# Scaling attention probabilities with one table of factors, and reading compression tokens at a stride

## The chip, the cores and the metric

The kernel runs on one core of one Trainium2 chip. The metric is device time of one execution, in microseconds (us); the text compares medians of several runs. The kernel is one program of about 16,000 instructions on five engines: TensorE (PE, with its weight loads listed apart as PEld), VectorE (DVE), ScalarE (ACT), GpSimd (POOL) and SyncE (SP), which issues most of the transfers.

## What is computed

Two layers of a transformer on 256 tokens of width 1024, in float32. The first layer mixes with a gated recurrence (HGRN2), the second with a sparse attention (NSA) whose keys and values come from a shared projection; each is followed by a gated feed-forward network. The change touches the second layer only, in two places:

```python
# compression of keys and values: blocks of 32 tokens, a new one every 16
r = t.reshape(B, S // CMP_STRIDE, CMP_STRIDE, NSA_KV_HEADS, NSA_HEAD_DIM)
blocks = jnp.concatenate([r[:, j:j + n_cmp] for j in range(n_sub)], axis=2)
blocks = blocks + pos[None, None, :, None, :]
flat = blocks.transpose(0, 1, 3, 2, 4).reshape(B, n_cmp, NSA_KV_HEADS, CMP_BLOCK * NSA_HEAD_DIM)
return jax.nn.silu(flat @ w1) @ w2
...
# attention: three branches, each a softmax, weighted by gates
g = g.reshape(B, Q_BLOCK, N_BRANCH, NSA_KV_HEADS, NSA_GROUP)[..., None]
o = g[:, :, 0] * o_c + g[:, :, 1] * o_s + g[:, :, 2] * o_w
```

With 256 tokens there are 15 compressed blocks for each of four key heads, and the selected and the windowed branch see all tokens up to the query's.

## The kernel before

Activations are held transposed, 128 features by 256 tokens. A float32 product is made of three TensorE products: every weight tile and every activation is split into a rounded part (`wh`, `hh`, written by ScalarE) and a remainder (`wl`, `hl`, written by VectorE at L308 and L480), and L484, L485 and L486 add `hh*wh`, `hl*wh` and `hh*wl`. So TensorE can start a weight tile only when ScalarE has copied it and VectorE has subtracted, 1024 columns at a time.

Weights stream through four buffers of 1 MB (`raw`), issued by SyncE in a fixed list; a buffer is loaded again when its last reader is done. The order of everything else comes from a scheduling framework, which places instructions on each engine by priorities and its own estimates; on the chip each engine then runs its list strictly in that order.

The second layer (`nsa`) goes as follows. Two projections make the tokens that are compressed (kind 0 keys, kind 1 values) and two more the selected and windowed keys `KR`. Then the list `ORDER["nsa"]` runs: `c` is compression, `q` a query projection (`nq`, four of them, into `QR`), `G` the gates, `n` the norm of two query projections (sums `hs`, a root made by ACT and DVE in turns into `hry` and `hrt`, then the products `hb`), `w` values, `x` the compressed branch's softmax (`css`, its transpose `pct`), `s` the scores of one pair of heads, `v` that pair's values, `a` parts of a modulation product.

The lines that the change touches are these. `cmp_blocks` (L1072 on) turns a projection into `Z`, 128 partitions by four heads by 128, then adds position vectors and stores blocks in `D`, one contiguous column group of 64 (four heads by 16 blocks) for each of 16 token offsets; column 15 of each head is cleared. `compress` (L1094 on) multiplies each such group as weights with 256 columns of `raw` (L1103), in two halves, kinds 0 and 1 on two halves of the array; each half frees its two `raw` buffers. `attend_scores` makes for each of eight pairs `j` two tiles `Pt` (one for each head of the pair): L1213 adds the mask and takes the maximum, ACT takes the exponential in eight instructions (L429), L1225 and L1227 make the factors `cf`, L1231 scales. `attend_values` transposes `Pt` on TensorE (`ptt`, L1246), copies it (L1249, L1251) and multiplies with the values (`po`, L1263).

Of the kernel before, what the change touches and what calls it, by code (L numbers as in the profile page):

```python
# [10 lines left out]
F32 = mybir.dt.float32  # L11
# [5 lines left out]
ALU = mybir.AluOpType  # L17
# [3 lines left out]
P = 128  # L21
S = 256
D = 1024
# [8 lines left out]
PTS = 3  # L32
# [164 lines left out]
class K:  # L197
# [767 lines left out]
    def nsa(self):  # L965
        nc = self.nc
        with self.tc.tile_pool(name="ns", bufs=1) as sp, self.tc.tile_pool(name="ns2", bufs=2) as s2, \
# [17 lines left out]
            KR = sp.tile([P, 2, 2, S], F32, name="KR")  # L985
            V = sp.tile([P, 2, 2, 256], F32, name="V")
            self.KR, self.V = KR, V
            Dt = [sp.tile([P, 16, 64], F32, tag=f"D{i}", name=f"D{i}") for i in range(2)]
            with self.tc.tile_pool(name="nsk", bufs=1) as sk:
                dk = []  # L990
                for kind in range(2):
# [18 lines left out]
                for kind in range(2):  # L1010
                    self.cmp_blocks(*dk[kind], kind, Dt[kind], sk)
                hk = self.full_pair(0, "kv", xr, s2, KACT)
            self.s3 = self.late.enter_context(self.tc.tile_pool(name="nsp", bufs=2 * PTS))
            self.QR = sp.tile([P, 8, S], F32, name="QR")

            self.QN, self.O = {}, None
# [18 lines left out]
            for t in ORDER["nsa"]:  # L1035
                n = int(t[1:] or 0)
# [22 lines left out]
            for i in range(4):  # L1059
                ws = self.fetch("nsa_out", i)  # L1060
                ps = self.acc_tile(f"nso{i}")
# [9 lines left out]
    def cmp_blocks(self, sw, u, kind, Dt, pool):  # L1071

        nc = self.nc
        Z = pool.tile([P, 4, P], F32, tag="Z", bufs=1, name=f"Z{kind}")
        for m in range(2):
            for hh in range(2):
                for par in range(2):
                    src = u[hh * 64:hh * 64 + 64, m].rearrange("p (t two) -> p two t", two=2)[:, par]
                    dst = Z[par * 64:par * 64 + 64, 2 * m + hh]
                    b = sw[hh * 64:hh * 64 + 64, m:m + 1]  # L1080
                    if par == 0:
                        nc.scalar.activation(dst, src, AF.Identity, bias=b)
                    else:
                        nc.vector.tensor_scalar_add(dst, src, b)
        nc.gpsimd.memset(Dt.rearrange("p i (h c) -> p i h c", h=4)[:, :, :, 15:16], 0.0)
        zv = Z.rearrange("p h (a r) -> p r h a", r=8)
        for half in range(2):
            d = Dt[:, 8 * half:8 * half + 8].rearrange("p i (h c) -> p i h c", h=4)[:, :, :, 0:15]
            pos = self.col(f"pos{kind}")[:, 8 * half:8 * half + 8][:, :, None].to_broadcast([P, 8, 15])
            for h in range(4):  # L1090
                nc.vector.tensor_tensor(d[:, :, h], zv[:, :, h, half:half + 15], pos, op=ALU.add)

    def compress(self, Dt):
        nc, tp = self.nc, self.tp  # L1094
        ps = self.m_tile([P, 256], "cmp1")
        for half in range(2):
            if half:
                yield
            raw = [self.fetch_raw("w1", 2 * half + kind) for kind in range(2)]
            w = [t.rearrange("p (i c) -> p i c", i=8) for _, t in raw]  # L1100
            for i in range(8):
                for kind in range(2):
                    nc.tensor.matmul(ps[64 * kind:64 * kind + 64], lhsT=Dt[kind][:, 8 * half + i], rhs=w[kind][:, i],  # L1103
                                     start=half == 0 and i == 0, stop=half == 1 and i == 7,
                                     tile_position=(0, 64 * kind))
            for n, _ in raw:
                self.release_raw(n)
        hid = self.pt_tile("hid")[:, :256]
        self.sigmoid(hid, ps, [P, 256])
        nc.vector.tensor_tensor(hid, ps, hid, op=ALU.mult)  # L1110
        self.cmp_tail(hid)
        yield
# [82 lines left out]
    def attend_scores(self, j):  # L1195
        nc, s2 = self.nc, self.s2
        g = j // 4
        mx = s2.tile([P, 8], F32, tag="mx", name="mx")
        sm = s2.tile([P, 8], F32, tag="sm", name="sm")
        Pt = [self.s3.tile([P, 2, 384], F32, tag="Pt", name=f"Pt{j}_{h}") for h in range(2)]  # L1200
        self.Pt[j] = Pt
        cs = self.c("caus")
        for tt, (o, n) in enumerate(((0, P), (P, S))):

            ps = [self.m_tile([P, 2, n], f"s{tt}") for _ in range(2)]
            for half in range(2):
                hs = slice(64 * half, 64 * half + 64)
                nc.tensor.matmul(ps[half], lhsT=self.QR[hs, j, tt * P:tt * P + P], rhs=self.KR[hs, g, :, 0:n],  # L1208
                                 start=True, stop=True)
            for br in range(2):  # L1210
                for half in range(2):
                    i = half * 4 + br * 2 + tt
                    nc.vector.tensor_tensor_reduce(out=Pt[half][:, br, o:o + n], in0=ps[half][:, br], in1=cs[:, S - n:],  # L1213
                                                   scale=1.0, scalar=-3e38, op0=ALU.add, op1=ALU.max,
                                                   accum_out=mx[:, i:i + 1])
        nm = s2.tile([P, 8], F32, tag="nm", name="nm")
        nc.vector.tensor_scalar_mul(nm, mx, -0.125)  # L1217
        for br in range(2):
            for half in range(2):
                for tt, (o, n) in enumerate(((0, P), (P, S))):  # L1220
                    i = half * 4 + br * 2 + tt
                    self.act(Pt[half][:, br, o:o + n], Pt[half][:, br, o:o + n], AF.Exp, scale=0.125,
                                         bias=nm[:, i:i + 1], accum_out=sm[:, i:i + 1])
        cf = s2.tile([P, 2, 2, 2], F32, tag="cf", name="cf")
        nc.vector.reciprocal(cf.rearrange("p a b c -> p (a b c)"), sm)  # L1225
        for tt in range(2):
            nc.vector.tensor_tensor(cf[:, :, :, tt], cf[:, :, :, tt], self.G[:, tt, j, :, 1:3], op=ALU.mult)  # L1227
        for br in range(2):
            for half in range(2):
                for tt, (o, n) in enumerate(((0, P), (P, S))):  # L1230
                    nc.vector.tensor_scalar_mul(Pt[half][:, br, o:o + n], Pt[half][:, br, o:o + n],  # L1231
                                                cf[:, half, br, tt:tt + 1])

    @first("av")
    def attend_values(self, j):
# [149 lines left out]
```

## Time and profile before

| what | value |
|---|---|
| median of three runs | 758.28 us (756.89 to 758.37) |
| profiled execution, its own time | 757.06 us |
| span of its profile | 755.3 us |
| TensorE busy | 727.8 us, 96% of the span |
| VectorE busy | 572.4 us, 76% |
| ScalarE busy | 394.9 us, 52% |
| mean TensorE clock granted | 0.993 of full |

Times below are us from the start of the span. A row of the timeline gives start, length, engine, line, operation, output and inputs with the number of instructions merged; in brackets stands how long the engine sat idle before, and what released it. Successive instructions of one engine overlap a little, so that one row's length is more than the step to the next row's start; the step is what an instruction costs in a busy queue.

### The profile page before, as it was taken

How to read it: one execution, taken by the hardware profiler on the slowest of the kernel's cores; microseconds unless marked ns; L12 is line 12 of the kernel's file. 1: busy time of each engine (PE TensorE's matmuls, PEld its weight loads, DVE VectorE, ACT ScalarE, POOL GpSimd, SP SyncE). 2: the span in 40 equal slices, each digit the busy share in tenths (PEclk: the TensorE clock that was granted, in tenths of full speed). 3: DMA queues.
4: the chain of work that ended last, by engine and by line, in shares of the span. 5: the costliest groups of instructions: out<-in, count | busy, mean ns of one | idle time of the engine just before them, and what ended most of it. 6: DMA issues, size and time to landing. Idle time of an engine off the chain costs nothing.

```text
span 755.3 us, 15991 instructions
## 1 busy us (share of the span) xinstructions
PE 727.8 (96%) x6580; PEld 663.9 (88%) x6580; DVE 572.4 (76%) x1231; ACT 394.9 (52%) x746; POOL 0.6 (0%) x7
## 2 busy tenths in 40 slices
PE   4999999899999999999999899999999999999997
PEld 2999986689999999999997787554799999999997
DVE  6996988459899898887679888679589657565641
ACT  4339856357645544544465654568566544544330
POOL 0000000000000000000000000000000000000000
PEclk9999999799999999999999999999999999999999
DMA  8999735375489797886744843453764646765700
GB/s 342 336 344 357 275 128 212 126 285 209 164 288 377 284 357 266 338 328 260 292 139 133 315 161 111 168 201 141 279 228 158 223 167 229 273 209 194 272 31 22
DMA packets 26571, 174.13 MB, mean 231 GB/s; under 512 B 3201, under 2 KB 4609, under 8 KB 6018
## 3 DMA queue, kind: packets, MB, share of 16 engines
q1 hardware_dynamic: 24912, 170.80, 61.6%
q10 hardware_dynamic: 1586, 2.32, 1.1%
q8 instruction: 51, 0.84, 0.4%
q14 instruction: 22, 0.18, 0.1%
HBM read 170.48 MB, written 1.05 MB: 227 GB/s over the span
## 4 chain that ended last, share of the span: by engine, by line
PE 88%; DVE 5%; ACT 3%; DMA 2%; issue 1%; ACTq 0%; DVEq 0%
PE ff L486 11%; PE ff L485 11%; PE ff L484 11%; PE ffo L484 6%; PE ffo L485 5%; PE ffo L486 5%; PE po L1263 3%; PE adapsss L385 2%; PE ptt L1246 2%; DVE wl L308 2%; PE s L1208 1%; PE adapsg L385 1%; PE q L485 1%; PE nso L484 1%; PE hg_i L748 1%
## 5 line engine op out<-in xcount | busy, mean ns | idle before, releaser
L308 DVE TENSOR_TENSOR wl<-raw,wh 128x1024 fp32r<-128x1024 f32 x201 | 243.7, 1220 | 71.9 <-ACT wh L307 71.6
L307 ACT CAST wh<-raw 128x1024 fp32r<-128x1024 f32 x201 | 208.4, 1048 | 155.4 <-PE ff L485 56.9
L486 PE MATMUL ff<-hh,wl 128*128 128x256 f32 (+1 forms) x704 | 198.3, 282 | 0.0
L485 PE MATMUL ff<-hl,wh 128*128 128x256 f32 (+1 forms) x704 | 198.1, 282 | 0.0
L484 PE MATMUL ff<-hh,wh 128*128 128x256 f32 (+1 forms) x704 | 198.1, 282 | 0.0
L486 PEld LDWEIGHTS ff<-hh,wl 128*128 128x128 f32 x704 | 133.1, 189 | 0.0
L485 PEld LDWEIGHTS ff<-hl,wh 128*128 128x128 f32 x704 | 132.7, 189 | 0.3
L484 PEld LDWEIGHTS ff<-hh,wh 128*128 128x128 f32 x704 | 132.6, 189 | 0.1
L484 PE MATMUL ffo<-gh,wh 128*128 128x256 f32 x352 | 99.4, 283 | 0.7 <-DVE x L638 0.7
L486 PE MATMUL ffo<-gh,wl 128*128 128x256 f32 x352 | 98.7, 281 | 0.8 <-DVE wl L308 0.8
L485 PE MATMUL ffo<-gl,wh 128*128 128x256 f32 x352 | 98.6, 280 | 0.0
L359 DVE CUSTOM_DVE_ANT_0 junk<-raw,crep 128x1024 f32<-128x1024 f32 x64 | 78.0, 1219 | 5.2 <-DMA raw<-in_w 4.6
L484 PEld LDWEIGHTS ffo<-gh,wh 128*128 128x128 f32 x352 | 66.1, 188 | 1.8 <-DVE x L638 1.5
L486 PEld LDWEIGHTS ffo<-gh,wl 128*128 128x128 f32 x352 | 66.1, 188 | 1.0 <-DVE wl L308 1.0
L485 PEld LDWEIGHTS ffo<-gl,wh 128*128 128x128 f32 x352 | 66.1, 188 | 0.0
L479 ACT CAST gh<-fg 128x256 fp32r<-128x256 f32 x44 | 17.8, 405 | 41.8 <-DVE fg L894 41.2
L429 ACT ACTIVATE Pt<-Pt,nm 128x128 f32<-128x128 f32 x64 | 28.2, 442 | 9.8 <-DVE nm L1217 9.8
L480 DVE TENSOR_TENSOR gl<-fg,gh 128x256 fp32r<-128x256 f32 x44 | 18.5, 421 | 8.2 <-ACT gh L479 8.2
L587 ACT ACTIVATE hh<-t,mod 128x256 fp32r<-128x256 f32 x24 | 11.3, 505 | 21.3 <-DVE t L586 21.3
L385 PE MATMUL adapsss<-raw,c 128*32 128x512 f32 x128 | 21.0, 629 | 1.0 <-issue 1.0
L429 ACT ACTIVATE fs<-ff 128x256 f32<-128x256 f32 x38 | 14.4, 379 | 14.1 <-PE ff L486 14.1
L638 DVE SCALAR_TENSOR_TENSOR x<-ffo,mod,x 128x256 f32<-128x256 f32 x16 | 7.7, 480 | 18.4 <-PE ffo L486 18.4
(322 smaller groups left out, 1463.8 us busy)
## 6 DMA issues: line engine op xcount, KB each, us to landing
raw<-in_w SPq DMA_DIRECT2D x160, 1024.0 KB, 6.2
x<-in_x SPq DMA_DIRECT2D x2, 512.0 KB, 4.9
usq<-huq ACTq DMA_DIRECT2D x16, 64.0 KB, 2.4
out<-x SPq DMA_DIRECT2D x8, 128.0 KB, 1.9
cst<-in_cst ACTq DMA_DIRECT2D x1, 558.0 KB, 6.6
usk<-huk ACTq DMA_DIRECT2D x8, 64.0 KB, 4.1
raw<-in_w SPq DMA_DIRECT2D x1, 512.0 KB, 4.3
rselr<-in_rsel SPq DMA_DIRECT2D x1, 256.0 KB, 2.8
```

The source lines that it names most:

```text
L307: nc.scalar.copy(wh, u)
L308: nc.vector.tensor_tensor(wl, u, wh.bitcast(F32), op=ALU.subtract)
L359: nc.vector.tensor_tensor_reduce(out=junk, in0=t[:, h * D:(h + 1) * D], in1=self.crep, scale=1.0, scalar=0.0, op0=ALU.mult, op1=ALU.add, a ...
L385: nc.tensor.matmul(self.aps[32 * j:32 * j + 32, :q], lhsT=self.c32[:, k], rhs=t[:, n * D + j * q:n * D + (j + 1) * q], start=k == 0, stop= ...
L429: r = nc.scalar.activation(out, in_, func, **kw)
L479: self.nc.scalar.copy(hi, v)
L480: self.nc.vector.tensor_tensor(lo, v, hi.bitcast(F32), op=ALU.subtract)
L484: mm(ps, lhsT=wh, rhs=hh, start=first, stop=False)
L485: mm(ps, lhsT=wh, rhs=hl, start=False, stop=False)
L486: mm(ps, lhsT=wl, rhs=hh, start=False, stop=last)
L1246: nc.tensor.transpose(pt[:, e], Pt[half][:, br, e * P:(e + 1) * P], self.c("ident"))
L1263: nc.tensor.matmul(po[64 * half:64 * half + 64, t], lhsT=w[:, half], rhs=rhs, start=n == 0, stop=n == len(steps) - 1, tile_position=(0, 64 ...
```

## The change

Three edits. Positions are added to whole rows of tokens: `Z` plus a position vector repeated over 64 groups of eight tokens, 128x512 at a time, once for each half, so that `D` holds all tokens in their order and nothing is cleared any more. The weights of the compression products are then taken from `D` by an access pattern, 64 columns that lie eight floats apart, the second half starting eight floats on. And the two `Pt` tiles of a pair become one, of which VectorE multiplies each branch in a single `tensor_tensor` with a small table of factors (two heads by three column blocks, repeated over 128 columns); the pool holds three of these tiles instead of six of half the size.

```diff
-            Dt = [sp.tile([P, 16, 64], F32, tag=f"D{i}", name=f"D{i}") for i in range(2)]
+            Dt = [sp.tile([P, 2, 512], F32, tag=f"D{i}", name=f"D{i}") for i in range(2)]
...
-            self.s3 = self.late.enter_context(self.tc.tile_pool(name="nsp", bufs=2 * PTS))
+            self.s3 = self.late.enter_context(self.tc.tile_pool(name="nsp", bufs=PTS))
...
-        nc.gpsimd.memset(Dt.rearrange("p i (h c) -> p i h c", h=4)[:, :, :, 15:16], 0.0)
-        zv = Z.rearrange("p h (a r) -> p r h a", r=8)
         for half in range(2):
-            d = Dt[:, 8 * half:8 * half + 8].rearrange("p i (h c) -> p i h c", h=4)[:, :, :, 0:15]
-            pos = self.col(f"pos{kind}")[:, 8 * half:8 * half + 8][:, :, None].to_broadcast([P, 8, 15])
-            for h in range(4):
-                nc.vector.tensor_tensor(d[:, :, h], zv[:, :, h, half:half + 15], pos, op=ALU.add)
+            pos = self.col(f"pos{kind}")[:, 8 * half:8 * half + 8][:, None, :].to_broadcast([P, 64, 8])
+            nc.vector.tensor_tensor(Dt[:, 1 - half].rearrange("p (a r) -> p a r", r=8),
+                                    Z.rearrange("p h (a r) -> p (h a) r", r=8), pos, op=ALU.add)
+
+    def block_cols(self, Dt, half, i):
+
+        return bass.AP(tensor=Dt.tensor, offset=Dt.offset + (8 if half else 512) + i,
+                       ap=[list(Dt.ap[0]), [P, 4], [8, 16]])
...
-                    nc.tensor.matmul(ps[64 * kind:64 * kind + 64], lhsT=Dt[kind][:, 8 * half + i], rhs=w[kind][:, i],
+                    nc.tensor.matmul(ps[64 * kind:64 * kind + 64], lhsT=self.block_cols(Dt[kind], half, i), rhs=w[kind][:, i],
...
-        Pt = [self.s3.tile([P, 2, 384], F32, tag="Pt", name=f"Pt{j}_{h}") for h in range(2)]
-        self.Pt[j] = Pt
+        PT = self.s3.tile([P, 2, 2, 384], F32, tag="Pt", name=f"Pt{j}")
+        Pt = self.Pt[j] = [PT[:, h] for h in range(2)]
...
-        cf = s2.tile([P, 2, 2, 2], F32, tag="cf", name="cf")
-        nc.vector.reciprocal(cf.rearrange("p a b c -> p (a b c)"), sm)
-        for tt in range(2):
-            nc.vector.tensor_tensor(cf[:, :, :, tt], cf[:, :, :, tt], self.G[:, tt, j, :, 1:3], op=ALU.mult)
+
+        rs = s2.tile([P, 2, 2, 2], F32, tag="rs", name="rs")
+        nc.vector.reciprocal(rs.rearrange("p a b c -> p (a b c)"), sm)
+        cf = s2.tile([P, 2, 2, 3], F32, tag="cf", name="cf")
+        for tt, e in ((0, 1), (1, 2)):
+            sh = [P, 2, 2, e]
+            nc.vector.tensor_tensor(cf[:, :, :, tt:tt + e], rs[:, :, :, tt:tt + 1].to_broadcast(sh),
+                                    self.G[:, tt, j, :, 1:3, None].to_broadcast(sh), op=ALU.mult)
         for br in range(2):
-            for half in range(2):
-                for tt, (o, n) in enumerate(((0, P), (P, S))):
-                    nc.vector.tensor_scalar_mul(Pt[half][:, br, o:o + n], Pt[half][:, br, o:o + n],
-                                                cf[:, half, br, tt:tt + 1])
+            v = PT[:, :, br].rearrange("p h (e t) -> p h e t", e=3)
+            nc.vector.tensor_tensor(v, v, cf[:, :, br, :, None].to_broadcast([P, 2, 3, P]), op=ALU.mult)
```

The scheduling framework places the instructions of the second layer anew. On VectorE, ahead of the first query's remainders (`wl_0_5340` before, `wl_0_5326` now), nothing is taken out but the eight position additions of kind 0, for which two now stand; behind them, both remainders stand ahead of the last `u` (L630), of which one stood ahead and one behind. Three other places matter below.

On VectorE behind the compression products: `sg` and `hid` are the sigmoid of the compression's hidden layer, `wl_0` of `raw_5337` (now `raw_5323`) belongs to the gates, that of `raw_5347` (now `raw_5333`) to the second query. Before:

```order
L470 TENSOR_SCALAR sg<-cmp_5318 128x256
L940 TENSOR_TENSOR QR<-QR,usq_5402 128x512
L308 TENSOR_TENSOR wl_0_5485<-raw_5337,wh_0_5484 128x1024
L480 TENSOR_TENSOR hl_5280<-t_5305,hh_5279 128x256
L480 TENSOR_TENSOR hl_5280<-t_5309,hh_5279 128x256
L308 TENSOR_TENSOR wl_0_5529<-raw_5347,wh_0_5528 128x1024
L474 TENSOR_SCALAR hid<-hid 128x256
L308 TENSOR_TENSOR wl_1_5533<-raw_5347,wh_1_5532 128x1024
L475 RECIPROCAL hid<-hid 128x256
```

And now:

```order
L470 TENSOR_SCALAR sg<-cmp_5304 128x256
L308 TENSOR_TENSOR wl_0_5471<-raw_5323,wh_0_5470 128x1024
L939 SCALAR_TENSOR_TENSOR usq_5388<-usq_5388,cols,cst 128x512
L474 TENSOR_SCALAR hid<-hid 128x256
L940 TENSOR_TENSOR QR<-QR,usq_5388 128x512
L475 RECIPROCAL hid<-hid 128x256
L308 TENSOR_TENSOR wl_0_5515<-raw_5333,wh_0_5514 128x1024
L476 TENSOR_TENSOR hid<-hid,sg 128x256
```

The reciprocal has moved ahead of the second query's remainder.

On TensorE among the products of the first values `v` (weights 0 and 1 alternate, twelve products each): `gt` is the transposed gate table, `hs` the sums of the first and second query. Before:

```order
L748 MATMUL v_5699<-wh_1_5704,hh_5279 128x256
L749 MATMUL v_5699<-wl_1_5705,hh_5279 128x256
L750 MATMUL v_5699<-wh_1_5704,hl_5280 128x256
L748 MATMUL v_5699<-wh_1_5704,hh_5279 128x256
L1162 MATMUL gt<-cst,gu 128x128 x2
L950 MATMUL hs<-hsqq_5400,cst 32x256 x2
L950 MATMUL hs<-hsqq_5589,cst 32x256 x2
L749 MATMUL v_5699<-wl_1_5705,hh_5279 128x256
```

And now:

```order
L748 MATMUL v_5679<-wh_0_5680,hh_5265 128x256
L950 MATMUL hs<-hsqq_5386,cst 32x256 x2
L749 MATMUL v_5679<-wl_0_5681,hh_5265 128x256
L750 MATMUL v_5679<-wh_0_5680,hl_5266 128x256
L748 MATMUL v_5679<-wh_0_5680,hh_5265 128x256
L749 MATMUL v_5679<-wl_0_5681,hh_5265 128x256
L950 MATMUL hs<-hsqq_5575,cst 32x256 x2
L750 MATMUL v_5679<-wh_0_5680,hl_5266 128x256
```

The sums have moved from the fourth group of twelve (behind 40 products) into the first (the last of them behind 11).

On TensorE where the scores begin: `pct` is the transpose of the compressed branch's probabilities, `s` the first scores. Before:

```order
L748 MATMUL v_5943<-wh_1_5948,hh_5279 128x256
L749 MATMUL v_5943<-wl_1_5949,hh_5279 128x256
L750 MATMUL v_5943<-wh_1_5948,hl_5280 128x256
L748 MATMUL v_5943<-wh_1_5948,hh_5279 128x256
L1191 MATMUL pct<-cst,css 128x128 x2
```

And now:

```order
L748 MATMUL v_5917<-wh_0_5918,hh_5265 128x256
L749 MATMUL v_5917<-wl_0_5919,hh_5265 128x256
L1193 MATMUL pct<-cst,css 128x128 x2
L1210 MATMUL s_5646<-KR,QR 128x256
L1210 MATMUL s_5647<-KR,QR 128x256
```

Before, 16 products of the second values stood ahead of `pct`; now eight do.

## Rows read from the trace of the kernel before

**Rows 1.** The page: busy time by engine, and the chain that ended last, by engine.

```profile
PE 727.8 (96%) x6580; PEld 663.9 (88%) x6580; DVE 572.4 (76%) x1231; ACT 394.9 (52%) x746; POOL 0.6 (0%) x7
...
PE 88%; DVE 5%; ACT 3%; DMA 2%; issue 1%; ACTq 0%; DVEq 0%
```

**Rows 2.** Busy time of each engine in stretches of the second layer: length, then PE, PEld, DVE, ACT, POOL busy (instructions), granted clock, DMA share, GB/s.

```profile
400.00:410.00 10.00, 8.13 (x59) 6.44 (x58) 9.87 (x24) 5.17 (x15) 0.00 (x0) 1.00 0.18 36
...
420.00:430.00 10.00, 7.64 (x60) 6.10 (x57) 7.34 (x13) 8.20 (x15) 0.00 (x0) 1.00 0.99 394
...
440.00:450.00 10.00, 8.20 (x71) 7.41 (x70) 7.07 (x19) 5.40 (x11) 0.00 (x0) 1.00 0.26 106
...
480.00:535.00 55.00, 54.96 (x388) 29.04 (x377) 40.27 (x184) 33.97 (x117) 0.00 (x0) 1.00 0.59 219
```

**Rows 3.** TensorE's timeline at the places where it waits, from several answers.

```profile
407.30 0.39 PE L486 MATMUL nq<-hh,wl 128*128 128x256 f32 x1 [1.87 <-DVE wl L308]
...
413.62 0.40 PE L959 MATMUL hb<-hry,rsel 128*128 128x256 f32 x2
...
415.43 7.12 PE L1103 MATMUL cmp<-raw,D 128*64 128x256 f32 x62
...
424.10 0.39 PE L484 MATMUL gates<-hh,wh 128*128 128x256 f32 x1 [1.56 <-ACT wh L307]
...
425.36 0.38 PE L486 MATMUL gates<-hh,wl 128*128 128x256 f32 x1 [0.75 <-DVE wl L308]
...
447.96 0.50 PE L959 MATMUL hb<-hry,rsel 128*128 128x256 f32 x2 [1.80 <-ACT hry L479]
...
472.99 0.55 PE L1246 MATMUL ptt<-cst,Pt 128*128 128x128 f32 x3 [0.45 <-ACT V L1032]
```

**Rows 4.** Groups of instructions of the stretch 400 to 560, by line and shape: out and in, count, busy us, mean ns of one, idle before.

```profile
L1091 DVE TENSOR_TENSOR D<-Z,cols 128x120 f32<-128x120 f32 x13 | 4.3, 373 | 0.0
...
L961 DVE TENSOR_TENSOR QR<-QR,hb 128x512 f32<-128x512 f32 x4 | 2.7, 681 | 0.0
...
L1181 DVE TENSOR_TENSOR css<-css,cmx 128x256 f32<-128x256 f32 x2 | 0.8, 419 | 0.0
...
L1231 DVE TENSOR_SCALAR Pt<-Pt,cf 128x256 f32<-128x256 f32 x32 | 11.1, 347 | 0.0
...
L1231 DVE TENSOR_SCALAR Pt<-Pt,cf 128x128 f32<-128x128 f32 x32 | 9.0, 281 | 0.0
...
L1103 PEld LDWEIGHTS cmp<-raw,D 128*64 128x64 f32 x64 | 4.7, 137 | 2.4
...
L484 PEld LDWEIGHTS nq<-hh,wh 128*128 128x128 f32 x64 | 12.1, 189 | 1.1 <-issue 0.8 <-ACT wh L307 0.3
```

**Rows 5.** VectorE's timeline around the first query's remainders.

```profile
402.12 0.37 DVE L1091 TENSOR_TENSOR D<-Z,cols 128x120 f32<-128x120 f32 x1
402.41 0.74 DVE L938 SCALAR_TENSOR_TENSOR KR<-huk,cols,cst 128x512 f32<-128x512 f32 x1
...
406.03 1.22 DVE L308 TENSOR_TENSOR wl<-raw,wh 128x1024 fp32r<-128x1024 f32 x1
407.16 0.42 DVE L630 TENSOR_TENSOR u<-k,rstd 128x256 f32<-128x256 f32 x1
...
411.72 0.41 DVE L460 SCALAR_TENSOR_TENSOR hrt<-hs,hrt 128x256 f32<-128x256 f32 x1
```

**Rows 6.** SyncE's queue where the gates' and the second query's weights are issued, and ScalarE's copy that waits for the first of them.

```profile
418.71 0.87 SPq L287 DMA_DIRECT2D raw<-in_w  x2
...
423.00 1.05 ACT L307 CAST wh<-raw 128x1024 fp32r<-128x1024 f32 x1 [1.65 <-DMA raw<-in_w]
```

**Rows 7.** VectorE's timeline at the second query's first remainder and the reciprocal behind it.

```profile
427.20 1.22 DVE L308 TENSOR_TENSOR wl<-raw,wh 128x1024 fp32r<-128x1024 f32 x1 [1.07 <-ACT wh L307]
...
429.68 1.75 DVE L475 RECIPROCAL hid<-hid 128x256 f32<-128x256 f32 x1
```

**Rows 8.** The root of the first two queries: sums on TensorE, ScalarE's first and last step, and a step of VectorE that stands in its queue between.

```profile
441.14 0.64 PE L950 MATMUL hs<-hsqq,cst 128*32 128x256 f32 x8
...
441.85 0.47 ACT L429 ACTIVATE hry<-hs,eps 128x256 f32<-128x256 f32 x1 [0.24 <-PE hs L950]
...
444.06 0.75 DVE L939 SCALAR_TENSOR_TENSOR usq<-usq,cols,cst 128x512 f32<-128x512 f32 x1 [1.87 <-DMA usq<-huq]
...
447.50 0.41 ACT L479 CAST hry<-hrr 128x256 fp32r<-128x256 f32 x1 [2.66 <-DVE hrr L463]
```

**Rows 9.** The start of the scores: TensorE's second values, `pct` and the second pair's scores, ScalarE's first exponential and the copy of `V` behind the sixteenth; and, in the fifth pair or so, VectorE's scaling and the transposes that follow it.

```profile
458.99 0.28 PE L748 MATMUL v<-wh,hh 128*128 128x256 f32 x1
...
460.94 0.44 PE L1191 MATMUL pct<-cst,css 128*128 128x128 f32 x2
...
464.46 1.78 PE L1208 MATMUL s<-KR,QR 64*128 64x512 f32 x4 [0.68 <-DVE mx L1213]
...
465.34 0.40 ACT L429 ACTIVATE Pt<-Pt,nm 128x128 f32<-128x128 f32 x1 [5.06 <-DVE nm L1217]
...
472.37 0.56 ACT L1032 COPY V<-v 128x512 f32<-128x512 f32 x1
...
516.76 1.92 DVE L1231 TENSOR_SCALAR Pt<-Pt,cf 128x128 f32<-128x128 f32 x8
...
517.46 1.27 PE L1246 MATMUL ptt<-cst,Pt 128*128 128x128 f32 x9
```

## The prediction

> **What bounds the kernel now.** The page comes first: TensorE is busy for 96% of the span and the chain that ended last lies on it for 88% [rows 1]. So an edit counts only where TensorE waits, or if it makes a TensorE instruction longer. The table by stretches shows where it has something to gain: some 2 us of every ten are idle around 400, 420 and 440, all at a granted clock of 1.00, while from 480 to 535 it is busy for 54.96 of 55 us [rows 2]. TensorE's timeline then names each wait of that part [rows 3]: 1.87 us for the first query's remainder `wl`; at the gates 1.56 for ScalarE's `wh` and 0.75 for `wl`; 1.80 at 447.96 for the root `hry`; and 0.45 at 472.99 for ScalarE's copy of `V`. Last come the timelines of the engines waited for [rows 5 to 9].
>
> I follow the shift of TensorE against its own place before (minus is earlier) through these waits. What an instruction costs in a full queue is its length less about 0.08: 373 ns at 402.12 makes a step of 0.29 [rows 5].
>
> **First query.** Eight additions ahead of its remainder go out (8 × 0.29 = 2.34 us) and two come in. The trace has no addition of this form on `Z`; a tensor-tensor of 128x512 takes 681 ns, a step of 0.60 [rows 4], so 1.20 comes in. The old ones at 373 ns read every eighth float; a dense 120 elements would take about 280 ns, by the line through 256 elements in 419 and 512 in 681 (1.02 ns an element and 0.157) [rows 4]. The new ones read densely, and 0.60 is a fair value (bounds: 0.55, and 0.95 at the strided 1.8 ns an element). VectorE is busy for 9.87 of ten us there [rows 2], so `wl` moves from 406.03 to about 404.9 and TensorE goes on 1.15 earlier, still after a wait of 0.7.
>
> More than half of that is given back. Behind `wl` now stand the other remainder, `u`, two additions, `KR`, `usk`, `KR` and two instructions of 128x256: 1.13 + 0.34 + 1.20 + 0.66 + 0.66 + 0.60 + 0.67 = 5.3 us to the root's step `hrt`, where 4.56 lay between (407.16 to 411.72) [rows 5]. That step comes at 411.3, only 0.45 earlier, and the products `hb` at 413.62 [rows 3], which need what follows it, can't move by more than about 0.5. **Shift −0.5.**
>
> **Compression.** The 64 weight columns now lie 32 bytes apart. No weight load of the trace is like that. Before, 62 passes take 7.12 us, 0.115 each, behind loads of 137 ns [rows 3, 4], so the loads are hidden. Below: nothing changes. Above: the load stands bare. Its nearest row is the strided addition, (373 − 157)/120 = 1.8 ns an element, so 64 columns take 118 ns, a pass 0.233, and 62 passes 7.3 us more. I take it as nearly hidden, at 0.123 a pass, because a load of 128 columns at 189 ns [rows 4] hides behind products of the same 256 columns, which follow each other 0.12 apart in the second values (16 products from 458.99 to 460.94) [rows 9]. Of the half us that this costs, the second half falls into the wait of 1.56: the transfer that ends it is issued at 418.71 [rows 6], when the first half's buffers come free, and only the first 31 passes delay it. **Shift −0.25.**
>
> **Second query.** Ahead of its remainder VectorE now has the gates' remainder (1.14), `usq` (0.67), a step of 0.12 for `hid`, `QR` (0.60) and the reciprocal, 1.75 long [rows 7]. From ScalarE's `wh`, done at 424.05 [rows 6] and now at 423.8, that is 423.8 + 1.14 + 0.67 + 0.12 + 0.60 + 1.67 = 428.0, and the remainder ends at 429.2. Before, it ended at 428.42 [rows 7], and TensorE needed it no earlier than about then. A new wait: **shift +0.7**. Behind it are held the second query's other products and all its sums.
>
> **The root.** The sums `hs` ran at 441.14 and ScalarE took them at 441.85; VectorE reached `hrt` only behind `usq`, for whose transfer it stood until 444.06, and the cast of `hry` ended at 447.91 [rows 8], 6.1 us after the first step, 1.87 of them this wait. Now the sums stand 29 products (3.5 us) earlier, behind 11 instead of 40 of the first values, and the second `usq` stands behind the root on VectorE. With the shift of +0.7 they end near 439.0 instead of 441.8, and the root at 443.3 to 445.1; `hb`, reached before at 447.96 − 1.80 = 446.16, is reached at 446.16 + 0.7 less 16 products that have moved behind it (1.9), 445.0. The 1.80 goes. **Shift −1.1.**
>
> **The scores.** `pct` comes eight products (0.95) sooner, so scores and exponentials start 2.05 earlier than 465.34. The sixteen exponentials take 7.0 us and the copy of `V` ended at 472.93 [rows 9]; now at about 470.9. TensorE, 1.1 early, with 0.24 of its wait of 0.68 at 464.46 [rows 9] filled by two products, is at the third transposes at 471.2, where it now finds the copy done, instead of at 472.99 [rows 3]. **Shift −1.8.**
>
> **Scaling.** Eight instructions become two. Before, by the 347 and 281 ns a pair costs 4 × 0.27 + 4 × 0.20 = 1.88 us; a tensor-tensor of 768 elements is 768 × 1.02 + 157 = 940 ns, a pair 1.80 in two steps. A factor that is broadcast is no dearer as far as L1181 shows, whose second operand is broadcast too and which lies on the same line (419) [rows 4]. Eight pairs save 0.6 us of VectorE, which is idle for 15 of 55 us there [rows 2]: nothing. But the first branch's first transposes, released after two instructions (0.5), now wait for a whole one (0.94), 0.45 later. In the fifth pair TensorE follows the scaling by 0.7 (516.76, 517.46) [rows 9]; it would lose up to 0.35, and I take 0.2. **Sum −1.6**, on 757.06 of the profiled execution (span 755.3 and 1.76 around it): 755.5. The median lies 1.22 above that execution, so 756.7.
>
> **The rivals.** *The waits come back.* The 1.80 at 447.96 is replaced by an equal one, if the second query's sums need ScalarE's squares later than I say, or its other steps stand behind casts there; the shift after it stays +0.7, the scores start only 0.25 earlier, TensorE is at the third transposes at 472.99 as before, and with the scaling's 0.2 the whole comes to +0.2: 758.5. For it: ScalarE's cast at 447.50 waited 2.66 for VectorE [rows 8], so two engines must both be on time. Against: VectorE is idle for 3 of 10 us there [rows 2].
>
> *Bare strided loads.* This ends on the other side. If a pass takes p, the first 31 delay the gates' transfer by 31(p − 0.115), and all 62 delay TensorE by 62(p − 0.115) − 1.56. The gain of the rest is 1.85, so the change loses from p = 0.17 on; at 0.233 the shift is 5.8 − 1.85 = +3.9: 762.2. For it: the 373 ns. Against: 0.05 must be exceeded beyond a cover that hides 189 ns. [...]
>
> *A slow table.* If the broadcast factor costs 1.8 ns an element, an instruction takes 1.54 and a pair 3.0 us. The first transposes come 1.0 late instead of 0.45; at 0.3 a pair for the seven pairs behind the first, 2.1 us are lost: net +0.3 or more, about 759. L1181 speaks against.
>
> *Nothing given back.* If the root is not held by VectorE and the reciprocal stays hidden, the first 1.15 stays whole and the +0.95 falls away: −3.2, 755.1.
>
> **Chances.** Forecast 0.52 (756.7; bounds of its terms 755.3 to 757.9), waits come back 0.20, bare loads 0.13, slow table 0.07, nothing given back 0.08. About 0.2%, 1.5 us, can be told from no change, so the border is 756.8. The forecast puts 0.34 below it and 0.18 within; returning waits are same, but for 0.02 slower; loads and table give 0.20 slower. Faster 0.42, same 0.36, slower 0.22. The range from 754.9, just below the last rival, to 760.5 leaves out half of the bare loads and the far ends.
>
> **What would show it.** In the changed trace: the first query's third product near 406.2 and `hb` near 413.1; 62 passes in 7.1 to 7.6 us; the second query's third product after a wait of over a us; no wait at the second `hb`; the first exponential near 463.3; `Pt` at 940 ns, `D` at 680. I am wrong if the passes take over 10 us, if a wait of over 1 us stands again at the second `hb`, or if TensorE waits for `Pt` in every pair.

## The result, and the profile after

The changed kernel takes 752.59 us (median of 6 runs, 748.16 to 755.09) against 758.49 (6 runs, 756.89 to 761.06): ratio 0.9924, 95% interval 0.9901 to 0.9948. It is 5.9 us faster; forecast were 1.6, in a range whose lower end was 754.9. Two repetitions gave 0.9944 (0.9922 to 0.9965) and 0.9934 (0.9912 to 0.9956), so 4 to 6 us is the size to be explained. The profiled execution has a span of 750.9, 4.4 less than before.

The page after, busy time and chain, to be held against [rows 1]: TensorE does the same 6580 products in the same 727.7 us.

```profile
PE 727.7 (97%) x6580; PEld 667.9 (89%) x6580; DVE 569.8 (76%) x1171; ACT 397.1 (53%) x746; POOL 0.4 (0%) x5
...
PE 88%; DVE 7%; ACT 2%; DMA 2%; issue 1%; ACTq 0%; DVEq 0%
```

The stretches of [rows 2], after:

```profile
400.00:410.00 10.00, 8.67 (x69) 7.37 (x68) 9.87 (x20) 5.35 (x14) 0.00 (x0) 1.00 0.44 140
420.00:430.00 10.00, 6.87 (x41) 6.06 (x39) 7.33 (x10) 6.04 (x8) 0.00 (x0) 0.83 1.00 407
440.00:450.00 10.00, 10.00 (x84) 9.84 (x84) 7.04 (x13) 5.07 (x10) 0.00 (x0) 1.00 0.40 127
480.00:535.00 55.00, 54.55 (x391) 30.64 (x390) 41.06 (x151) 36.03 (x118) 0.00 (x0) 1.00 0.63 233
```

Less is idle around 400 and nothing around 440, but more around 420, where the granted clock is now 0.83. The last line is the one to remember: TensorE is as busy as before (54.55 of 55 us against 54.96), and yet it will turn out to have been faster there.

TensorE's waits after, to be held against [rows 3]:

```profile
404.49 0.39 PE L486 MATMUL nq<-hh,wl 128*128 128x256 f32 x1 [1.33 <-DVE wl L308]
...
411.36 0.50 PE L959 MATMUL hb<-hry,rsel 128*128 128x256 f32 x2 [0.42 <-ACT hry L479]
...
413.34 7.18 PE L1105 MATMUL cmp<-raw,D 128*64 128x256 f32 x62
421.92 0.38 PE L484 MATMUL gates<-hh,wh 128*128 128x256 f32 x1 [1.40 <-ACT wh L307]
423.19 0.58 PE L486 MATMUL gates<-hh,wl 128*128 128x256 f32 x1 [0.76 <-DVE wl L308]
...
428.67 0.39 PE L486 MATMUL nq<-hh,wl 128*128 128x256 f32 x1 [0.97 <-DVE wl L308]
...
444.93 0.40 PE L959 MATMUL hb<-hry,rsel 128*128 128x256 f32 x2
...
462.76 1.44 PE L1210 MATMUL s<-KR,QR 64*128 64x512 f32 x4 [0.59 <-DVE mx L1215]
...
470.33 1.20 PE L1250 MATMUL ptt<-cst,Pt 128*128 128x128 f32 x9
```

The waits changed as forecast: 1.87 became 1.33, a new one of 0.97 stands at the second query, the 1.80 at the second `hb` and the 0.45 at the transposes are gone. But these rows alone don't give the gain. I aligned the two executions by how much of TensorE's work was done; the shift of after against before runs like this (us, minus is earlier):

| TensorE is at | shift |
|---|---|
| end of the first layer's feed-forward, 345 | −0.3 |
| start of the second layer, 360 to 400 | −1.8 |
| behind the first query, 412 | −2.8 |
| compression, 418 to 421 | −2.0 |
| second query, 431 | +0.2 |
| behind the second `hb`, 449 to 456 | −1.0 |
| attention, 475 | −2.0 |
| 500 | −2.4 |
| output projection, 545, and to the end | −4.2 |

Two of its steps lie where no wait of the forecast is: 1.5 us between 345 and 360, in code that is the same in both, and 2.2 in the attention, above all in its last ten us.

### The profile page after: what moved, and what is told of

It reads as the page before. It is cut to its first block, busy times and chain, and to the rows that moved or that the text cites. A ratio compares the mean times of both kernels' runs of the same rounds, so it can differ in the third digit from the quotient of the medians.

```text
span 750.9 us, 15924 instructions
## 1 busy us (share of the span) xinstructions
PE 727.7 (97%) x6580; PEld 667.9 (89%) x6580; DVE 569.8 (76%) x1171; ACT 397.1 (53%) x746; POOL 0.4 (0%) x5
## 4 chain that ended last, share of the span: by engine, by line
PE 88%; DVE 7%; ACT 2%; DMA 2%; issue 1%; ACTq 0%; DVEq 0%
PE ff L486 11%; PE ff L485 11%; PE ff L484 11%; PE ffo L484 6%; PE ffo L485 6%; PE ffo L486 6%; PE adapsss L385 2%; PE po L1267 2%; PE ptt L1250 2%; DVE wl L308 2%; PE s L1210 1%; PE q L485 1%; PE q L486 1%; PE nso L484 1%; PE hg_i L748 1%; PE adapsg L385 1%
```

## The experiments

The first four tell apart three theories: B, as predicted (all of the gain in the waits of the compression part, none in the scaling); A, that the scaling part shortens the attention by way of TensorE's order; C, that the step at 345 to 360 is chance.

**Before and after once more.**

> The kernel before, unchanged, profiled once more. The profile of before lost 1.76 us against that of after between 341 and 358 us, in the first layer's feed-forward, whose code is the same in both: a load of weights landed 1.7 us later and TensorE waited 0.78 us for wl. If that is chance (theory C: a part of the measured gain is not the edits'), this profile shows no such wait and its span is about 753.5; if it belongs to this kernel's program, the wait stands there again. Time within 0.3% of before.

Ratio 1.0006 (0.999 to 1.0021). In the first profile of before, VectorE stood 2.64 us for a transfer, which made TensorE late:

```profile
348.47 1.23 DVE L359 CUSTOM_DVE_ANT_0 junk<-raw,crep 128x1024 f32<-128x1024 f32 x1 [2.64 <-DMA raw<-in_w]
...
355.44 0.39 PE L486 MATMUL ffo<-gh,wl 128*128 128x256 f32 x1 [0.78 <-DVE wl L308]
```

In after the same instruction waited 0.95:

```profile
346.48 1.23 DVE L359 CUSTOM_DVE_ANT_0 junk<-raw,crep 128x1024 f32<-128x1024 f32 x1 [0.95 <-DMA raw<-in_w]
```

In the second profile of before TensorE doesn't wait there, and from 345 to 360 it gains the same 1.5 us on the first profile. Theory C holds for this step: of the 4.4 between the two profiles, 1.5 are the first profile's bad luck. But the span was 756.2, not the 753.5 expected: the 1.5 was lost again at 405 and 1.2 more around 450, of which below.

> The changed kernel once more, 5 rounds. All theories: a ratio near 0.993. Its profile had the clock at half between about 423.5 and 425.2 us, after TensorE's waits at the gates; if that is chance it is gone here and the second query starts about 0.8 earlier than in the first profile of after.

Ratio 0.9944 (0.9922 to 0.9965). The half clock was not gone; it came later, from 429 on, as TensorE came out of the second query's wait, which was 1.93 this time.

**One part alone.** The two edits of the diff, one at a time.

> Only the compression part (positions on whole rows, weights at a stride); Pt as before. As predicted (theory B) the whole gain is here, about -1.8 us. Theory A (the gain lies in the attention, where TensorE's list of instructions changes less often between transposes and value products, which only the Pt part brings about): here only what the two traces show up to the scores, -0.6 to -1.0 us, and TensorE's list has 14 changes from transposes to value products, as before.

Ratio 0.9963 (0.9942 to 0.9983): −2.8 us, with bounds −4.4 and −1.3: more than theory A left for it (−0.6 to −1.0).

> Only the Pt part (one tile, two multiplications); compression as before. Theory B: +0.2 us, at most a few tenths either way. Theory A: 9 such changes instead of 14, and TensorE goes through the scores and values about 1.9 to 2.3 us faster than before (-1.8 to -2.3 us in all), though VectorE saves only 0.06 us a pair.

Ratio 0.9975 (0.9959 to 0.9991): −1.9 us (−3.1 to −0.7). The parts multiply to 0.9938, as the whole. So the compression part does somewhat more than forecast and the scaling part, forecast at +0.2, does −1.9, as theory A has it; theory B falls. VectorE is not why: the scaling costs what was said, 953 ns an instruction (rows of after).

```profile
L1236 DVE TENSOR_TENSOR Pt<-Pt,cf 128x768 f32<-128x768 f32 x16 | 14.6, 953 | 0.2
...
L1105 PEld LDWEIGHTS cmp<-raw,D 128*64 128x64 f32 x64 | 6.7, 198 | 0.7
...
L1087 DVE TENSOR_TENSOR D<-Z,cols 128x512 f32<-128x512 f32 x2 | 1.3, 680 | 0.0
```

And TensorE did lose 0.42 at the fifth pair, as feared (0.35), in after:

```profile
514.76 1.82 DVE L1236 TENSOR_TENSOR Pt<-Pt,cf 128x768 f32<-128x768 f32 x2
```

```profile
515.87 0.85 PE L1250 MATMUL ptt<-cst,Pt 128*128 128x128 f32 x6 [0.42 <-DVE Pt L1236]
```

What it gained is in the order of its list. Before, near the end of the attention (transposes `ptt` use the whole array, 128*128; value products `po` half of it, 128*64):

```profile
530.69 0.44 PE L1246 MATMUL ptt<-cst,Pt 128*128 128x128 f32 x2
531.06 0.65 PE L1263 MATMUL po<-PT,V 128*64 128x256 f32 x2
531.64 0.33 PE L1246 MATMUL ptt<-cst,Pt 128*128 128x128 f32 x1
531.90 0.43 PE L1263 MATMUL po<-PT,V 128*64 128x128 f32 x2
532.26 0.33 PE L1246 MATMUL ptt<-cst,Pt 128*128 128x128 f32 x1
532.52 0.43 PE L1263 MATMUL po<-PT,V 128*64 128x128 f32 x2
```

After, at the same place:

```profile
527.77 0.60 PE L1267 MATMUL po<-PT,V 128*64 128x128 f32 x4
528.30 0.66 PE L1250 MATMUL ptt<-cst,Pt 128*128 128x128 f32 x4
528.89 0.43 PE L1267 MATMUL po<-PT,V 128*64 128x128 f32 x2
529.25 0.44 PE L1250 MATMUL ptt<-cst,Pt 128*128 128x128 f32 x2
```

Read the starts: one transpose and two products in turn take 0.26 + 0.36 us; four transposes in a row take 0.59. No row shows a wait. From the first `pct` to the first `nso` the list of before goes 14 times from transposes to values and 10 times back, that of after 9 and 6 times; counted by the part of the array that is used, 71 changes became 64, with the Pt part alone 62. Before and the Pt part alone have the same 522 products there, so their steps can be added up: those into another part of the array took 21.34 us before and take 19.77, all others 54.85 and 54.58.

**The order alone.** The transposes get a higher priority in the kernel before; every instruction stays.

```diff
-                for e in range(3):
-                    nc.tensor.transpose(pt[:, e], Pt[half][:, br, e * P:(e + 1) * P], self.c("ident"))
+                with self.tc.high_priority(offset=10):
+                    for e in range(3):
+                        nc.tensor.transpose(pt[:, e], Pt[half][:, br, e * P:(e + 1) * P], self.c("ident"))
```

> The kernel before with one change of order and no change of any instruction: the transposes of Pt get a higher priority, so that TensorE's list has 8 changes from transposes to value products instead of 14 and 4 back instead of 10 (all changes between kinds of products from the first pct on: 71 instead of 74). VectorE keeps its eight scalings a pair. Theory A (the attention is faster because of fewer changes on TensorE): 0.8 us (by all changes, at 1.83 us for the 7 that the Pt part saved) to 2.4 us (by those between transposes and values, at 1.83 us for 9) off between the first pct and the output projection. Rival D (the Pt part gains because VectorE has fewer instructions and gives way): no gain here, 0 to +0.5 us.

From the first `pct` to the output projection 74.50 us against 76.20 and 76.19: −1.70, within theory A's bounds, with the eight scalings in place and 56 changes of the array's part. The ratio is 0.9979 (0.9965 to 0.9994). Rival D falls.

> The same priority in the changed kernel: 8 changes from transposes to value products instead of 9, one back instead of 6, but 78 changes of all kinds instead of 69. Theory A in its narrow form (only changes between transposes and values cost): -0.5 to -1.2 us against the changed kernel. In its wide form (every change costs alike): +1 to +2.4 us.

74.27 us against 73.94, and 0.9963 (0.995 to 0.9976): +0.33 in the attention. But eight value products have moved behind the first `nso`, out of this stretch; from the first `pct` to the end of the span the run is 1.5 us longer than after, of which 0.2 are waits. So the narrow form falls, and the time is in the wide form's range (+1 to +2.4). That every change costs alike does not hold, though: a change of kind on the same part of the array made no step longer: 0.11 us from `adat` to a transpose and 0.113 from one transpose to the next, in the rows of the block below. Counted by the array's part the changes to the end are 70 against 64, some 0.2 us each.

**The price of a change by itself.** At the end of the attention, 24 extra transposes and 24 extra pairs:

```diff
+            for f in [xtt, xpo] * 24:      # the other run: [xtt] * 24 + [xpo] * 24
+                f()
```

> The kernel before with 24 extra transposes of a Pt block and 24 extra pairs of value products of 128 columns at the end of the attention, whose results nobody reads: one transpose, one pair, in turn. Its block against that of the next run is the price of the changes alone. Theory A: 0.26 us for a transpose and 0.36 for a pair, as the rows of the profile of before at 531.6 to 532.5 us have them, so some 15 us for the block, against 6 in groups. Rival: the rows there are long because of waits for data, and the block takes about 6 us in both.

In turn, a few periods:

```profile
535.40 0.33 PE L1271 MATMUL xtt<-cst,Pt 128*128 128x128 f32 x1
535.66 0.44 PE L1275 MATMUL xpo<-PT,V 128*64 128x128 f32 x4
536.03 0.33 PE L1271 MATMUL xtt<-cst,Pt 128*128 128x128 f32 x1
```

> The same 24 transposes and 24 pairs, first all transposes, then all pairs. Theory A: about 24 x 0.11 + 24 x 0.14 = 6 us, some 8 to 9 us less than in turn. Rival: the same as in turn, within 1 us.

```profile
536.56 0.55 PE L1246 MATMUL ptt<-cst,Pt 128*128 128x128 f32 x3
536.94 0.38 PE L396 MATMUL adat<-cst,adasm 128*128 128x128 f32 x2
537.16 2.78 PE L1271 MATMUL xtt<-cst,Pt 128*128 128x128 f32 x24
539.87 5.45 PE L1275 MATMUL xpo<-PT,V 128*64 128x128 f32 x94
545.26 0.33 PE L396 MATMUL adat<-cst,adasm 128*128 128x128 f32 x1
```

A period in turn is 0.63 us (535.40 to 536.03); in groups a transpose is 0.113 and a pair 0.23 (0.11 and 0.14 were expected). The block takes 16.2 us in turn (533.04 to 549.26) and 9.3 in groups (535.99 to 545.26): 7.0 us for 46 changes, 0.15 us a change, with the same operands for all, ready from the first on, and no wait in the rows (expected were 15 and 6 us, 8 to 9 apart). The whole runs, one of each, were 771.78 and 767.73, 4.0 apart, since the second one came to the block 3.0 later.

From `adat` to the extra transposes, another kind on the same part of the array, the step is 0.11 us (two from 536.94 to 537.16), as from one transpose to the next. And in the attention itself a change costs as much as in the block or more. With the waits of the stretch set apart (1.17 us before, 1.59 with the Pt part alone, 1.82 with the order alone), the Pt part gains 2.3 us by 9 changes fewer and the order alone 2.4 by 15: 0.25 and 0.16 each.

**One tile, old scaling.**

> The kernel before with one Pt tile for a pair and three of them in the pool, but the old eight scalings. TensorE's list in the attention has the same number of changes as before (74, of which 14 and 10 between transposes and values). Theory A: no difference to before, within 0.2%, and 76.2 us from the first pct to the output projection as before. Rival E (one tile for a pair, or its fewer buffers, is what helps): 1.8 us off, as with the whole Pt part.

Ratio 0.9993 (0.9975 to 1.0012), 76.18 us, with 71 changes of the array's part as before: nothing. Rival E falls. It is neither the tile nor its buffers, but the instructions of the scaling, by which the framework then places the transposes otherwise.

**The new wait.** In after the reciprocal stands ahead of the second query's remainder, as forecast, behind a `usq` that waits for its transfer:

```profile
424.32 0.75 DVE L939 SCALAR_TENSOR_TENSOR usq<-usq,cols,cst 128x512 f32<-128x512 f32 x1 [1.19 <-DMA usq<-huq]
...
425.79 1.74 DVE L475 RECIPROCAL hid<-hid 128x256 f32<-128x256 f32 x1
427.46 1.16 DVE L308 TENSOR_TENSOR wl<-raw,wh 128x1024 fp32r<-128x1024 f32 x1
```

The edit ties it behind the remainder (and emits the end of the compression behind the second query):

```diff
+            nc.vector.tensor_scalar(one, self.last_w[2][0][1].bitcast(F32)[:, 0:1], 0.0, 1.0, op0=ALU.mult, op1=ALU.add)
+            nc.vector.tensor_scalar_add(hid, hid, one)
             nc.vector.reciprocal(hid, hid)
```

> The changed kernel with the compression's reciprocal tied behind the second query's first remainder: the 1 that is added ahead of it comes from a column computed from that remainder (0 x wl + 1), and the end of the compression is emitted behind the second query, so that VectorE's list has both remainders ahead of the reciprocal. The sums hs move from behind 11 products of the first values to later ones. If the reciprocal makes the new wait at the second query (0.97, 1.93 and 0.86 us in the three profiles of kernels with the stride part), that wait falls to 0.3 or less and the time by 0.6 to 1.5 us against the changed kernel, less what a later root gives back at the second hb. Rival: the wait is set by ScalarE's wh and the transfer, and stays.

```profile
426.41 2.35 DVE L308 TENSOR_TENSOR wl<-raw,wh 128x1024 fp32r<-128x1024 f32 x2
...
429.25 1.75 DVE L1125 RECIPROCAL hid<-hid 128x256 f32<-128x256 f32 x1
```

TensorE has no wait at the second query, so the reciprocal made it. But the time is 0.9937 (0.9914 to 0.9959), no better than the changed kernel's 0.9924 to 0.9944: the 0.6 to 1.5 us that were expected of it did not come.

> The changed kernel a third time, on the same chip as the next run, to compare the two: ratio 0.992 to 0.996. Its profile has the second query's wait of 0.9 to 2 us again and one stretch at half clock between 420 and 435 us.

> The kernel with the late reciprocal once more. By the traces (from the end of the compression's products to the first pct 37.98 us, against 38.80 and 40.69 in the changed kernel) it is 0.8 to 2.7 us faster than the run before this one; if the wait that it removes is made up for elsewhere, the two are equal within 0.2%.

On one chip after gave 0.9934 (0.9912 to 0.9956), its wait at the second query 1.92, and the late reciprocal 0.9928 (0.9907 to 0.995), with 0.24 there:

```profile
428.57 0.39 PE L486 MATMUL nq<-hh,wl 128*128 128x256 f32 x1 [1.92 <-DVE wl L308]
```

```profile
426.67 0.39 PE L487 MATMUL nq<-hh,wl 128*128 128x256 f32 x1 [0.24 <-DVE wl L308]
```

In the traces the new order is ahead by 1 to 3 us at `pct`, with ten more of the values' products done; the medians, 752.71 and 752.76, don't show it. Part of that is the draw: of the changed kernel the profiled execution was the slowest of its six (754.53), of the late reciprocal one below the median (751.79). And between the first `nso` and the end the late one is 0.8 us longer (215.3 against 214.5). The rest stays open, and no version that beats the changed kernel came out.

**All profiles by stage.** Worked out from the starts of TensorE's rows: from the first product of `kv` to the last `cmp`, on to the first `pct`, on to the first `nso`; and where a stretch at half clock (granted clock 0.50) began between 400 and 465.

| kernel | to `cmp` | to `pct` | to `nso` | half clock from |
|---|---|---|---|---|
| before | 50.85 | 38.77 | 76.20 | |
| before again | 52.35 | 40.14 | 76.19 | 407, 448 |
| one tile | 52.29 | 39.21 | 76.18 | 405 |
| Pt only | 52.30 | 38.43 | 74.35 | 405 |
| order, before | 50.87 | 42.15 | 74.50 | 425, 449 |
| alternating | 50.88 | 41.33 | | 423, 447 |
| grouped | 52.31 | 41.66 | | 406, 426, 450 |
| stride only | 50.57 | 38.98 | 75.79 | 425 |
| after | 50.59 | 38.80 | 73.94 | 423 |
| after again | 50.58 | 40.69 | 73.95 | 429 |
| after, third | 50.56 | 40.67 | 73.95 | 429 |
| order, after | 50.60 | 38.86 | 74.27 | 426 |
| late reciprocal | 50.60 | 37.98 | 73.28 | 425 |
| the same again | 50.62 | 37.68 | 73.86 | 463 |

The upper seven have the old compression. The kernels with the new one, but for the late reciprocal, do eight products of the values behind `pct` instead of ahead of it, so their last two columns count together. The Pt part is worth 76.19 − 74.35 = 1.84. The compression part, as the mean of the upper seven against the five between "stride only" and "order, after": 51.69 to 50.58, 40.24 to 39.60, and 76.19 to 75.79, together 2.2 us.

## Why the prediction was wrong

**First query: right.** The additions take 680 ns (681 forecast). TensorE was 1.08 earlier behind it (1.15), though only 0.54 of that is the shorter wait; six sums `hs` ahead of it, 1.15 us long before, took 0.63. Up to the compression 0.27 was left (0.5 forecast).

**Compression: right, and its rival dead.** 62 passes take 7.18 us against 7.12 [rows 3], 0.116 each where 0.123 was taken. The loads did become longer, 198 ns against 137 [rows 4], about 0.95 ns a column more. Why they did, no row shows. What the longer loads cost the kernel is next to nothing, as the passes show (0.116 us against 0.115).

**Second query and root: right waits, wrong sum.** The wait came (0.86 to 1.93 in five profiles) and the 1.80 went, but TensorE was some 0.8 later than before at 456 (from 400 on), where 1.1 earlier was forecast. Three things were not in the sum: the stretch at half clock; that `usq` waits for its transfer ahead of the reciprocal (1.19), which I had as ready; and that the sums `hs`, now in two groups of four with two more changes of the array's part, take 0.8 us more with the steps into and out of them (1.5 against 0.8).

**Scores: right by luck.** The first exponential started at 463.29 (463.3 forecast), but 1.8 of its 2.05 us were gained ahead of all that the change touches, 1.5 of them by the chance of the first profile. Counted from the first product of `kv` it comes after 93.73 us against 94.02, and after 95.6 in the two later profiles of the same kernel. The third transposes did not wait, as forecast.

**Scaling: the step that failed.** "Eight pairs save 0.6 us of VectorE, which is idle for 15 of 55 us there [rows 2]: nothing", and 0.2 lost: the instructions cost what was said (1.82 a pair, 1.80 forecast) and the loss at the fifth pair came. But I took TensorE's list in the attention as given. The new instructions made the framework place 9 runs of transposes among the values instead of 14, and at 0.15 us or more a change (9 fewer by the array's part) that is worth more than the 0.6 us that VectorE saves. The term was +0.2 and measured −1.84 in the trace and −1.9 in time. None of the three signs by which I would have called myself wrong came; none of them looked at the order. I read [rows 2], 54.96 of 55 us busy, as "nothing to gain", but the changes of the array's part, 0.15 us or more each, are inside the busy time.

**The clock: not in the sum at all.** Seven profiles with the old compression have 11 stretches at half clock between 400 and 465, the seven with the new one 7. The difference is those from 405 to 407: behind the first query's wait, 1.87 in all seven of the old, four have one, and it costs 1.44 us (52.31 against 50.87 to `cmp`); behind the shorter wait of the new (1.32 to 1.34) none has. At 0.57 a run that is 0.8 of the compression part's 2.2, as far as seven profiles of each can tell. The profile of before that I worked from had none at all, so nothing in it pointed there.

Put together from the profiles: −2.2 for the compression part, of which −0.8 are the clock and −1.4 stand where −1.8 were forecast, and −1.8 for the order are −4.0. That is less than the three comparisons gave (5.9, 4.2 and 5.0), but within the interval of each (3.9 to 7.5, 2.7 to 5.9, 3.3 to 6.7). Why the first gave most is not settled. The compression part's 2.2 is a mean of profiles; against the one profile of before that the forecast was made from it is 0.6.

## What to carry to other kernels

- When a framework orders the instructions, compare the whole list of the bound engine before and after, not only the places where it waits: count how often it changes between shapes of the array, at a price measured in this kernel (0.15 us or more a change here).
- "Busy 100%" is no proof that nothing can be gained (54.96 of 55 us were busy here, and the Pt part still made the attention 1.84 us shorter); take the step from one start to the next, grouped by what comes next.
- One profile of a kernel that waits is one draw: profile it twice before a 1 us difference is read from it.

## What the runs showed of the hardware

A change between products on the whole array and on half of it cost 0.15 us (46 changes, 7.0 us), with operands ready and no wait in the rows. What in such a change takes the time, no row shows.

The granted clock fell to 0.50 behind some waits of 0.69 to 1.93 us and not behind others of the same length. In after it is 0.50 from 423.0 to 426.0, and the products there start 0.21 us apart (423.57, 423.78, 423.99), against 0.12 from 426.47 on. The rows that follow give the mean over 5 us. Before, at the first query's and the gates' waits, in the first profile:

```profile
405.00:410.00 5.00, 3.13 (x20) 2.38 (x21) 4.97 (x10) 2.24 (x6) 0.00 (x0) 1.00 0.25 45
...
425.00:430.00 5.00, 4.59 (x36) 4.38 (x37) 3.87 (x7) 5.00 (x10) 0.00 (x0) 1.00 1.01 428
```

In the second profile of the same kernel, with the same wait of 1.87 at the first query and 1.90 at the second `hb`:

```profile
405.00:410.00 5.00, 4.69 (x24) 3.90 (x24) 5.00 (x11) 2.22 (x5) 0.00 (x0) 0.69 0.42 133
...
445.00:450.00 5.00, 3.10 (x19) 2.89 (x18) 4.51 (x10) 1.35 (x2) 0.00 (x0) 0.79 0.01 3
```

With the compression part alone, behind the waits of 1.53 and 0.76 at the gates:

```profile
425.00:430.00 5.00, 4.14 (x22) 3.94 (x21) 4.53 (x6) 4.03 (x4) 0.00 (x0) 0.66 1.01 421
```

And with the late reciprocal, second profile, behind 1.63 and 0.75, where it stayed up (it fell at 463 instead, after a wait of 0.69 at the scores):

```profile
425.00:430.00 5.00, 4.54 (x36) 4.34 (x37) 4.93 (x7) 3.91 (x6) 0.00 (x0) 1.00 1.00 416
```

The same wait brings it in one execution and not in the next, so what a wait costs can't be read from one profile: with such a stretch behind the first query's wait of 1.87 the way to `cmp` took 1.44 us more than without (52.31 against 50.87), and the late reciprocal took away one of 1.92 us without a gain in the median. What decides whether the clock falls was not tried.
